# Context inverses: key products one group a step behind U, vector slack of two gaps, another filling of the head

## The chip, the cores and the metric

The kernel runs on one NeuronCore of a Trainium2 chip. The core has five engines that work side by side, each through its own queue of instructions: PE (TensorE, matrix products), DVE (VectorE), ACT (ScalarE), POOL (GpSimd) and SP (SyncE, which here only issues DMAs). The metric is the device time of one execution in microseconds (us).

## The reference

One layer of a hybrid backbone: 1024 latent tokens with a prefix of 256 context tokens, model width 1024. A modulated RMSNorm feeds one wide input projection, whose columns go to two branches: bidirectional RWKV-7 time mixing (16 heads of 64) and bidirectional retention. Both give gated outputs that are merged, projected and added to the input. The change concerns the RWKV-7 scan over the context. Per token the reference does

```python
sa = jnp.einsum('bhvk,bhk->bhv', S, kk_t)
S = (S * w_t[:, :, None, :] - sa[..., None] * b_t[:, :, None, :]
     + v_t[..., None] * k_t[:, :, None, :])
```

The latent scan starts from the final state S of the context scan of the same direction.

## The kernel before

**Chunks.** The scan is done in chunks of 64 tokens: 4 for the context, 16 for the latent tokens. Within a chunk the recurrence becomes a triangular system, and each chunk, head and direction needs the inverse T2 of a 64 x 64 triangular matrix. The states then pass from chunk to chunk by a few small products. There are 8 pairs of heads and 2 directions.

**Inverses.** One inverse job (`inverse(n)`, line 806) handles 64 such matrices in three stages, and is a Python generator. Each `yield` is a place at which the caller puts other work.
- `inv_keys` (line 847): loads keys from DRAM and makes four groups of key products (tile B on PE, 32 matmuls in the trace's records for each group). ACT evicts each group, in twelve copies, to the tiles D (line 883) and T (line 885). The loads of a group are two of tile kt and four of tile bi, on the SP queue. The tiles kt and bi have two buffers each, and a group uses both, so the next group's loads wait until the products of the group before are done. It yields once after the first loads and once after each group.
- `inv_vec` (line 888): inverts the 32 x 32 diagonal blocks on DVE: transposes of D to E (line 896), 31 rounds of two operations on tmp and TL (lines 902 and 904), transposes to TD and TN (lines 908 and 912). E needs the whole of D, all four groups. The generator hands out estimated durations, 32.1 us in all, and `inverse` yields each time 4.2 us (`VEC`) have been handed out: seven times.
- `inv_join` (line 925): two rounds of small products (tile I on PE, 128 matmul records a round) with TN and T, with four evictions by ACT after each round (lines 944 and 946). All of TN is needed for the first. It yields after each round.

**Chain.** The context scan runs in two groups of 4 head pairs, and each in two halves: four calls of `chain_ctx` (line 1094). I call them runs 1 to 4. A run loads its operands and makes chunk products (A, bt), with projection work put between by `fill(2.0)`, and then takes 4 steps (`chain_step`, line 1042). A step is X on PE, copied by ACT to xs; U on PE, copied by ACT to uv; S on PE, added on DVE to the state sv (line 1083; send at the last step). Each waits for the one before. After each of the three products the step calls `step_inv`, which advances the current inverse to its next yield, and then `gap`, which fills the gap with projection work. Two runs have 24 such calls; what is left of the inverse then is done at once (`drain`).

**Which inverse runs where.** Inverse 0 is for the first group of the context; it runs ahead of run 1 with nothing but projection work beside it. I call this stretch the head. Inverse 1, for the second group, is advanced in runs 1 and 2. Inverse 2, for the first latent chunks, is advanced in runs 3 and 4. After run 4 the rest of the projection is done, and the latent part begins.

**Filling.** The projection work of this phase is 8 jobs of 240 matmuls (tile gv, 128 x 256) with the split of their weights into a high part (whi, ACT, line 659) and a low part (wlo, DVE, line 660). `fill(us)` emits matmuls by an estimate of 0.107 us each. In the head each yield gets 2.8 us (`HEAD`), the first 7.0 us. A `gap` gets an equal share of what is left, less 8 us (`HOLD`) kept for the end: `share = max(self.left - self.hold, 0.0) / max(self.gaps, 1)`, with 48 gaps in all. So what the head emits is taken from the gaps.

**Order.** PE executes in the order of the program: `mm` and `pin` chain each product to the one before. Vector work and evictions of the inverse are kept behind the last chain operation of their engine (`late`), and the chain's own operations have a higher priority for the scheduler (`URGENT`), so that they stand ahead of waiting vector work. SP, DVE and ACT keep the order that the scheduler gave them.

Of the kernel before, what the change touches and what calls it, by code (L numbers as in the profile page):

```python
# [50 lines left out]
HEAD = 2.8  # L51
# [77 lines left out]
class Kern:  # L129
# [676 lines left out]
    def inverse(self, n):  # L806

        job = {}
        for _ in self.inv_keys(n, job):
            yield  # L810
            yield
        us = 0.0
        for t in self.inv_vec(job):
            us += t
            if us > VEC:
                us = 0.0
                yield
        for _ in range(5):
            yield
        yield from self.inv_join(job)  # L820

    def rwkv_ctx(self):
        pds = [[(p, d) for p in range(4 * g, 4 * g + 4) for d in range(2)] for g in range(2)]
        for i, _ in enumerate(self.inverse(0)):
            self.fill(HEAD if i else 2.5 * HEAD)
        for g in range(2):
            self.inv = self.inverse(g + 1)
            for q in range(2):
                self.chain_ctx(pds[g][4 * q:4 * q + 4], self.t2[g][q])
            self.drain()  # L830
# [769 lines left out]
```

## Time and profile before

| what | value |
|---|---|
| runs shown | 2459.37 us median of 3 (2459.12 to 2461.17) |
| the profiled execution | 2467.66 us |
| its span, first to last instruction | 2465.6 us |
| mean granted clock of PE | 0.986 |
| the phase of the change, in the trace | 815.5 to 1154.9 us |
| head; run 1 (loading and steps); run 2; run 3; run 4 and rest | from 815.5; 917.1; 974.3; 1034.9; 1097.3 us |

A page of the profile gives the busy time of each engine and the chain of work that ended last. The trace behind it answers closer questions: sums over stretches of time, groups of instructions by line and tile, and the instructions of an engine in order of time, each with the idle time of the engine before it and what released it. Lines such as L902 are lines of the kernel. In names such as B<-kt,bi the tile that is written stands ahead of the arrow. The steps of run 4 begin at 1116.3 us, and its last U, at 1133.3 us, is followed by the first join of inverse 2.

### The profile page before, as it was taken

How to read it: one execution, taken by the hardware profiler on the slowest of the kernel's cores; microseconds unless marked ns; L12 is line 12 of the kernel's file. 1: busy time of each engine (PE TensorE's matmuls, PEld its weight loads, DVE VectorE, ACT ScalarE, POOL GpSimd, SP SyncE). 2: the span in 40 equal slices, each digit the busy share in tenths (PEclk: the TensorE clock that was granted, in tenths of full speed). 3: DMA queues.
4: the chain of work that ended last, by engine and by line, in shares of the span. 5: the costliest groups of instructions: out<-in, count | busy, mean ns of one | idle time of the engine just before them, and what ended most of it. 6: DMA issues, size and time to landing. Idle time of an engine off the chain costs nothing.

```text
span 2465.6 us, 55584 instructions
## 1 busy us (share of the span) xinstructions
PE 2356.7 (96%) x22224; PEld 1927.3 (78%) x22224; DVE 1570.7 (64%) x2774; ACT 1120.5 (45%) x2411; POOL 682.8 (28%) x852
## 2 busy tenths in 40 slices
PE   7999999999999999999999999999898998999998
PEld 4888888888888899988877787777666765688786
DVE  5486787786776153434777788776378557754644
ACT  6434344434444424344555555644366335533422
POOL 2221021112122122323234433434376345400000
PEclk9999999999999899989999999999999999999999
DMA  6154454454446525344667777766565655585542
GB/s 253 50 152 116 142 154 138 127 171 124 139 140 175 183 80 141 105 132 132 164 173 195 190 192 180 189 175 163 148 201 158 202 169 159 175 294 163 186 169 86
DMA packets 417908, 393.60 MB, mean 160 GB/s; under 512 B 217578, under 2 KB 320754, under 8 KB 414578
## 3 DMA queue, kind: packets, MB, share of 16 engines
q1 hardware_dynamic: 392818, 299.85, 41.5%
q0 software_dynamic: 23104, 87.05, 12.4%
q8 instruction: 175, 2.87, 0.5%
q10 hardware_dynamic: 1728, 3.15, 0.3%
q14 instruction: 83, 0.68, 0.1%
HBM read 268.82 MB, written 121.11 MB: 158 GB/s over the span
## 4 chain that ended last, share of the span: by engine, by line
PE 82%; DVE 5%; DMA 5%; issue 3%; ACT 2%; POOL 1%; SPq 1%; DVEq 0%; ACTq 0%; POOLq 0%
PE gm L557 10%; PE gm L330 9%; PE gm L331 9%; PE gm L332 9%; PE gv L557 9%; PE ro L1479 4%; PE A L557 3%; PE yr L1279 2%; PE yr L1280 2%; PE yr L1278 2%; PE X L557 2%; PE bt L1038 2%; PE S L557 1%; PE O L557 1%; PE I L557 1%
## 5 line engine op out<-in xcount | busy, mean ns | idle before, releaser
L330 PE MATMUL gm<-uh,wh 128*128 128x512 f32 x896 | 351.2, 393 | 6.2 <-ACT xp L402 4.2
L331 PE MATMUL gm<-ul,wh 128*128 128x512 f32 x896 | 351.6, 392 | 0.8 <-DVE ul L299 0.8
L332 PE MATMUL gm<-uh,wl 128*128 128x512 f32 x896 | 351.2, 392 | 0.0
L330 PEld LDWEIGHTS gm<-uh,wh 128*128 128x128 f32 x896 | 168.1, 188 | 40.7 <-ACT xp L402 4.6
L331 PEld LDWEIGHTS gm<-ul,wh 128*128 128x128 f32 x896 | 168.4, 188 | 37.9 <-issue 1.7
L332 PEld LDWEIGHTS gm<-uh,wl 128*128 128x128 f32 x896 | 168.3, 188 | 34.3
L557 PE MATMUL gm<-ul,whi 128*128 128x512 f32 x416 | 168.5, 405 | 1.6 <-issue 1.6
L557 PE MATMUL gm<-uh,wlo 128*128 128x512 f32 x416 | 166.8, 401 | 1.0 <-DVE wlo L660 1.0
L557 PE MATMUL gm<-uh,whi 128*128 128x512 f32 x416 | 166.7, 401 | 0.0
L660 DVE TENSOR_TENSOR wlo<-wraw,whi 128x256 fp32r<-128x256 f32 x168 | 82.4, 508 | 129.1 <-ACT whi L659 128.4
L557 PE MATMUL gv<-whi,uh 128*128 128x256 f32 x512 | 151.5, 296 | 0.0
L557 PE MATMUL gv<-whi,ul 128*128 128x256 f32 x512 | 149.7, 292 | 0.0
L557 PE MATMUL gv<-wlo,uh 128*128 128x256 f32 x512 | 149.1, 291 | 0.0
L211 DVE TENSOR_TENSOR lo<-raw,hi 128x512 fp32r<-128x512 f32 x128 | 92.9, 730 | 88.2 <-ACT hi L210 87.7
L210 ACT CAST hi<-raw 128x512 fp32r<-128x512 f32 x128 | 78.6, 620 | 142.7 <-PE yr L1279 78.1
L1060 POOL TENSOR_TENSOR sp<-sv,pc 64x512 f32<-64x512 f32 (+1 forms) x92 | 89.5, 973 | 175.4 <-DVE sv L1083 153.9
L904 DVE TENSOR_TENSOR TL<-TL,tmp 128x31 f32<-128x31 f32 (+15 forms) x310 | 125.9, 406 | 8.2
L1479 PE MATMUL ro<-s,rs 128*128 128x512 f32 x256 | 124.5, 599 | 5.1 <-DVE s L1433 4.6
L902 DVE TENSOR_TENSOR tmp<-E,TL 128x31 f32<-128x31 f32 (+15 forms) x310 | 117.0, 377 | 8.4
L210 ACT CAST wh<-wr 128x1024 fp32r<-128x1024 f32 x56 | 58.8, 1050 | 130.6 <-PE gm L331 103.0
L456 POOL DMA_DIRECT2D vtD<-vt x64 | 46.1, 767 | 240.5 <-ACT vt L452 240.5
L1433 DVE SCALAR_TENSOR_TENSOR s<-s,ph,st 128x512 f32<-128x512 f32 x128 | 91.1, 739 | 33.8 <-PE st L1420 29.0
(300 smaller groups left out, 6217.5 us busy)
## 6 DMA issues: line engine op xcount, KB each, us to landing
wr<-in_w_in SPq DMA_DIRECT2D x56, 512.0 KB, 3.7
wraw<-in_w_in SPq DMA_DIRECT2D x84, 256.0 KB, 4.0
bk<-bkD SPq DMA_DIRECT2D x80, 256.0 KB, 4.3
krD<-kr POOLq DMA_DIRECT2D x16, 1024.0 KB, 4.6
raw<-in_wr SPq DMA_DIRECT2D x64, 256.0 KB, 3.3
vtD<-vt POOLq DMA_DIRECT2D x64, 160.0 KB, 4.2
bkD<-bk POOLq DMA_DIRECT2D x32, 320.0 KB, 6.6
bkD<-bk POOLq DMA_DIRECT2D x16, 640.0 KB, 6.5
```

What stands on the lines that cost most here:

```text
L210: nc.scalar.copy(hi, src)
L211: (eng or nc.vector).tensor_tensor(lo, src, hi.bitcast(F32), op=ALU.subtract)
L330: nc.tensor.matmul(acc[:, :n], hi[:, k, :], self.hi(k, t0, n), start=(k == 0), stop=False)
L331: nc.tensor.matmul(acc[:, :n], hi[:, k, :], self.lo(k, t0, n), start=False, stop=False)
L332: nc.tensor.matmul(acc[:, :n], lo[:, k, :], self.hi(k, t0, n), start=False, stop=(k == KT - 1))
L557: return self.pin(self.nc.tensor.matmul(*a, **k))
L660: self.late(nc.vector.tensor_tensor(lo[:, j % size, k:k + 2], r, h.bitcast(F32), op=ALU.subtract), "v")
L902: self.late(nc.vector.tensor_tensor(t3, et[:, j + 1:, j:j + 1].broadcast_to([P, n, m]), tl[:, j:j + 1, 0:m].broadcast_to([P, n, m]), op=AL ...
L904: self.late(nc.vector.tensor_tensor(tl[:, j + 1:, 0:m], tl[:, j + 1:, 0:m], t3, op=ALU.subtract), "v")
L1060: nc.gpsimd.tensor_tensor(sp[ch], sv[ch, h], pcs[ch].broadcast_to([64, m, C]), op=ALU.mult)
L1433: nc.vector.scalar_tensor_tensor(new[:, k], old[:, k], self.cd[:, d, h:h + 1], a, op0=ALU.mult, op1=ALU.add)
L1479: nc.tensor.matmul(po, qx[d][:, k, cols], st[:, k, :], start=(d == 1 and k == 0), stop=False)
```

## The change

Three numbers change. In `inverse`, the yields after the stages of `inv_keys` become 4, 3, 3, 3 and 1 in place of 2 each; the pause between vector work and join becomes 2 yields in place of 5. In `rwkv_ctx`, the filling of the head becomes 2.8 us for each of its first 14 pieces and 1.7 times as much, 4.76 us, for those after them, in place of 7.0 us for the first and 2.8 for the rest.

```diff
-        for _ in self.inv_keys(n, job):
-            yield
-            yield
+        for i, _ in enumerate(self.inv_keys(n, job)):
+            for _ in range((4, 3, 3, 3, 1)[i]):
+                yield
...
-        for _ in range(5):
-            yield
+        yield
+        yield
         yield from self.inv_join(job)
...
-            self.fill(HEAD if i else 2.5 * HEAD)
+            self.fill(HEAD if i < 14 else 1.7 * HEAD)
```

Counted in calls of `step_inv`: before, the groups of key products came at calls 3, 5, 7 and 9 (all in the first of the two runs, behind S, U, X and S), the vector work from call 11 to 18, and the join at call 23 and 24. Now the groups come at calls 5, 8, 11 and 14 (behind U of steps 2, 3 and 4 of the first run and of step 1 of the second), the vector work from call 15 to 22, the first round of the join at call 24, behind the last S, and the second in the drain.

In numbers of projection products on PE: the four groups of the head are 52 or 53 products apart before and 78 or 79 now; between the last of them and the first join there were 366 and are 426; a gap of runs 1, 2, 3 and 4 held about 22, 19, 15 and 6 and now holds 18 or 19, 15 or 16, 10 or 11, and 2. After the first round of inverse 2's join there were 6 + 3 + 6 + 72 products, and now there are 6 + 5 + 66.

PE at the last group of key products of inverse 2. Before, run 3, step 3 (S of that step, then the group; gv are projection products):

```order
L557 MATMUL gv_10255<-whi_9149,uh_98 128x256
L557 MATMUL S_10297<-uv_10060,bt_9738 64x64 x2
L557 MATMUL S_10297<-uv_10060,bt_9774 64x64 x2
L557 MATMUL S_10297<-uv_10060,bt_9830 64x64 x2
L557 MATMUL S_10297<-uv_10060,bt_9871 64x64 x2
L557 MATMUL B_10308<-kt_10229,bi_10230 64x64 x2
L557 MATMUL B_10309<-kt_10234,bi_10235 64x64 x2
```

The same group now, in step 1 of run 4:

```order
L557 MATMUL X_10687<-sv_10467,ka_10567 64x64 x2
L557 MATMUL gv_10586<-whi_9567,uh_104 128x256
L557 MATMUL gv_10586<-wlo_9568,uh_104 128x256
L557 MATMUL U_10703<-xs_10696,T_883_8350 64x64 x8
L557 MATMUL B_10714<-kt_10406,bi_10407 64x64 x2
L557 MATMUL B_10715<-kt_10411,bi_10412 64x64 x2
```

The group moved from behind S in run 3, ahead of the chunk loading of run 4, to behind U in run 4.

PE at the first round of the join of inverse 2. Before, in the last step of run 4, where a gap holds six products:

```order
L557 MATMUL gv_10961<-whi_9793,uh_98 128x256
L557 MATMUL gv_10961<-wlo_9794,uh_98 128x256
L557 MATMUL gv_10961<-whi_9793,ul_106 128x256
L557 MATMUL gv_10961<-whi_9793,uh_99 128x256
L557 MATMUL gv_10961<-wlo_9794,uh_99 128x256
L557 MATMUL gv_10961<-whi_9793,ul_107 128x256
L557 MATMUL U_10986<-xs_10975,T_870_8126 64x64 x8
L557 MATMUL I_10997<-TN_10865,T_1081_9945 32x32 x2
L557 MATMUL I_10998<-TN_10865,T_1082_9946 32x32 x2
```

Now, at the same place of the program:

```order
L557 MATMUL gv_10748<-whi_9567,uh_102 128x256
L557 MATMUL gv_10748<-wlo_9568,uh_102 128x256
L557 MATMUL U_10994<-xs_10984,T_883_8350 64x64 x8
L557 MATMUL gv_10748<-whi_9567,ul_110 128x256
L557 MATMUL gv_10748<-whi_9567,uh_103 128x256
L557 MATMUL S_11007<-uv_10879,bt_10522 64x64 x2
L557 MATMUL S_11007<-uv_10879,bt_10558 64x64 x2
L557 MATMUL S_11007<-uv_10879,bt_10606 64x64 x2
L557 MATMUL S_11007<-uv_10879,bt_10645 64x64 x2
L557 MATMUL I_11018<-TN_10962,T_1086_10056 32x32 x2
L557 MATMUL I_11019<-TN_10962,T_1087_10057 32x32 x2
```

The join moved from behind the last U to behind the last S, and the gaps ahead of it shrank from six products to two.

DVE at the start of the vector work of inverse 2. Before, in run 3 (sv are the state adds of its second and third step, wlo a split of projection weights):

```order
L1083 TENSOR_TENSOR sv_10059<-S_10163,sp_10076 64x256 x2
L660 TENSOR_TENSOR wlo_9794<-wraw_9901,whi_9793 128x256
L660 TENSOR_TENSOR wlo_9794<-wraw_10089,whi_9793 128x256
L1083 TENSOR_TENSOR sv_10191<-S_10297,sp_10208 64x256 x2
L896 STREAM_TRANSPOSE E_10399<-D_9944 128x256 x4
L660 TENSOR_TENSOR wlo_9794<-wraw_10089,whi_9793 128x256
L902 TENSOR_TENSOR tmp_10406<-E_10399,TL_10400 128x31
```

Now, in run 4 (ka are masked chunk products of its loading, sv the state add of its first step):

```order
L1014 TENSOR_TENSOR ka_10524<-A_10594,mask 64x256 x2
L1014 TENSOR_TENSOR ka_10567<-A_10633,mask 64x256 x2
L1083 TENSOR_TENSOR sv_10681<-S_10750,sp_10698 64x256 x2
L896 STREAM_TRANSPOSE E_10761<-D_10055 128x256 x4
L902 TENSOR_TENSOR tmp_10768<-E_10761,TL_10762 128x31
L904 TENSOR_TENSOR TL_10762<-TL_10762,tmp_10768 128x31
```

The start of the vector work moved from behind the third step of run 3 to behind the first step of run 4, past the loading of run 4.

## The prediction

> **What bounds the kernel now.** The page comes first: how busy each engine is, and who holds the chain of work that ended last.
>
> ```profile
> PE 2356.7 (96%) x22224; PEld 1927.3 (78%) x22224; DVE 1570.7 (64%) x2774; ACT 1120.5 (45%) x2411; POOL 682.8 (28%) x852
> PE 82%; DVE 5%; DMA 5%; issue 3%; ACT 2%; POOL 1%; SPq 1%; DVEq 0%; ACTq 0%; POOLq 0%
> ```
>
> TensorE is the bound, and it runs its instructions in the order written. The change adds and removes no product; it only moves products between places. So the question is how much TensorE time the context phase loses, before and after. The second view gives sums over stretches of time (length, busy time and instructions of PE, PEld, DVE, ACT and POOL, granted clock, DMA share, GB/s). Its last row is the whole phase, from the first projection product to the first product of the latent part; the others are the stretches at half clock inside it that a stall began.
>
> ```profile
> 839.60:846.43 6.83, 5.26 (x46) 5.09 (x47) 0.00 (x0) 3.22 (x12) 0.00 (x0) 0.50 0.66 196
> 1068.30:1075.12 6.82, 6.41 (x61) 5.96 (x62) 0.83 (x2) 3.22 (x12) 0.00 (x0) 0.50 0.58 165
> 1085.36:1092.19 6.83, 5.58 (x57) 5.13 (x57) 1.51 (x3) 3.22 (x12) 0.30 (x1) 0.50 0.48 120
> 1136.56:1146.80 10.24, 9.97 (x233) 8.79 (x232) 0.84 (x2) 4.06 (x9) 3.15 (x4) 0.50 0.51 117
> 815.50:1154.86 339.36, 324.53 (x4160) 305.35 (x4160) 135.65 (x349) 133.15 (x360) 83.74 (x117) 0.94 0.44 123
> ```
>
> PE idles 339.36 - 324.53 = 14.8 us of the phase. Half of the busy time at half clock is lost as well: (5.26 + 6.41 + 5.58 + 9.97) / 2 = 13.6. Together **28.4 us** is lost now, and that is all the change could win here. The third view, PE's rows in order of time, says who is waited for (idle time and releaser in brackets). I call the four calls of chain_ctx runs 1 to 4, and the inverses 0 (head), 1 (beside runs 1 and 2) and 2 (beside 3 and 4).
>
> ```profile
> 830.42 0.69 PE L557 MATMUL B<-kt,bi 64*64 64x64 f32 x32
> ...
> 841.17 1.45 PE L557 MATMUL B<-kt,bi 64*64 64x64 f32 x28 [3.36 <-DMA bi<-bkD]
> 850.80 0.69 PE L557 MATMUL B<-kt,bi 64*64 64x64 f32 x32
> 857.85 0.69 PE L557 MATMUL B<-kt,bi 64*64 64x64 f32 x32
> 902.58 0.75 PE L557 MATMUL I<-TN,T 32*32 32x32 f32 x64
> ...
> 955.43 1.00 PE L557 MATMUL B<-kt,bi 64*64 64x64 f32 x28 [1.23 <-DMA bi<-bkD]
> ...
> 1066.42 0.32 PE L557 MATMUL B<-kt,bi 64*64 64x64 f32 x2 [0.33 <-DMA bi<-bkD]
> 1067.33 0.33 PE L557 MATMUL B<-kt,bi 64*64 64x64 f32 x2 [0.58 <-DMA bi<-bkD]
> 1068.71 1.11 PE L557 MATMUL B<-kt,bi 64*64 64x64 f32 x26 [1.06 <-DMA bi<-bkD]
> 1086.61 1.11 PE L557 MATMUL B<-kt,bi 64*64 64x64 f32 x26 [1.82 <-DMA bi<-bkD]
> 1135.85 0.94 PE L557 MATMUL I<-TN,T 32*32 32x32 f32 x64 [1.86 <-DVE TN L912]
> ```
>
> Two kinds of wait: key products (B) for their operands from DRAM, and once a join (I) for the vector work that ends in TN. At 1135.85 PE stood still although 6 and then 72 ready projection products were queued behind the join: what stands behind a blocked product waits too.
>
> **What the wider spacing is worth.** A group's loads start when the group before has freed the two buffers. From the end of one B (850.80 + 0.69) to the next at 857.85, 6.4 us was enough; the loads that ended the wait at 955.43 were begun after a B that ended some 8.5 us earlier.
>
> ```profile
> 947.14 0.40 SPq L839 DMA_DIRECT2D kt<-kcD  x1
> ```
>
> So a group needs 6.4 to 8.5 us. In the head the spacing goes from 52 products to 79. The 366 products from 858.54 to 902.58 took 0.120 us each, so this is 9.5 us, against the 10.1 us from the first B's end (831.11) to 841.17, where its SP queue still had run 1's loads to issue: I leave 0.5 us of the 3.36, and no half clock. In run 1 three gaps of 18 products give about 8.4 us: 0.5 us is left. In run 3 the gaps shrink, since the head has taken their filling. A gap with 15 products and one with 6:
>
> ```profile
> 1054.39 0.69 PE L557 MATMUL X<-sv,ka 128*64 128x64 f32 x16
> 1056.99 0.68 PE L557 MATMUL U<-xs,T 64*64 64x64 f32 x16
> ...
> 1121.12 0.69 PE L557 MATMUL X<-sv,ka 128*64 128x64 f32 x16 [0.17 <-issue]
> 1122.64 0.68 PE L557 MATMUL U<-xs,T 64*64 64x64 f32 x16
> ```
>
> These are 2.60 and 1.52 us. By the new order run 3 has 10 or 11 products a gap, 2.07 us; three gaps leave 6.2 us between groups, so two groups wait 0 to 2.3 us each. I take the middle, 1.2 each, **2.4 us**, and no half clock, as the single wait of 1.23 us brought none. Its other end, 7.5 us, is two full waits and one half-clock stretch (2.9).
>
> **What the later last group costs.** The vector work starts from D, which the last group fills. Before, inverse 2's last group stood behind S in run 3, and the chunk loading of run 4 lay within the vector work's time. A sum over its stretch (length, PE busy, clock, DMA):
>
> ```profile
> 1097.20:1116.20 19.00, 19.00 (x203) 1.00 0.41 116
> ```
>
> This is 19 us of PE work that no longer covers it. The last group now stands behind U of the first step of run 4; inverse 1's likewise in run 2. How long the vector work takes, from the groups of DVE in the stretch of inverse 2 (busy, mean ns, idle before), then of inverse 0:
>
> ```profile
> L904 DVE TENSOR_TENSOR TL<-TL,tmp 128x31 f32<-128x31 f32 (+15 forms) x31 | 12.0, 388 | 1.0
> L902 DVE TENSOR_TENSOR tmp<-E,TL 128x31 f32<-128x31 f32 (+15 forms) x31 | 11.8, 380 | 0.9
> L1083 DVE TENSOR_TENSOR sv<-S,sp 64x256 f32<-64x256 f32 x6 | 2.5, 422 | 4.0 <-PE S L557 3.9
> L908 DVE STREAM_TRANSPOSE TD<-TL 128x256 f32<-128x256 f32 x4 | 2.4, 626 | 0.0
> L896 DVE STREAM_TRANSPOSE E<-D 128x256 f32<-128x256 f32 x4 | 2.2, 597 | 6.4 <-ACT D L883 6.4
> L912 DVE STREAM_TRANSPOSE TN<-TL 128x256 f32<-128x256 f32 x4 | 2.1, 614 | 0.0
> ...
> L902 DVE TENSOR_TENSOR tmp<-E,TL 128x31 f32<-128x31 f32 (+15 forms) x31 | 10.6, 343 | 1.0
> L660 DVE TENSOR_TENSOR wlo<-wraw,whi 128x256 fp32r<-128x256 f32 x10 | 3.8, 418 | 2.4 <-ACT whi L659 2.4
> ...
> 1090.68 2.15 DVE L896 STREAM_TRANSPOSE E<-D 128x256 f32<-128x256 f32 x4 [6.41 <-ACT D L883]
> ```
>
> Inverse 2: 12.0 + 11.8 + 2.4 + 2.2 + 2.1 + 1.9 between them = 32.4 us; inverse 0, with 10.6 in place of each of the two long rows, 30.1. I take **31**, and both ends for the range. E began 3.0 us after its last B ended (1086.61 + 1.11 = 1087.72), when ACT had evicted D.
>
> Inverse 2, from the end of its last B: 3.0 + 31 + three pairs of state adds (sv, sv, send) at 0.85 = 36.6 us to TN. By the new order a gap of run 4 holds 2 products: 1.52 - 4 x 0.12 = 1.04 us of PE work. Ten gaps to the end of run 4 are 10.3 us, and then the join is next on PE. So PE loses **26.3 us**, some 9 in run 4 (where X waits for a state add behind vector work on DVE) and the rest at the join. The second join product now follows the first directly and waits for ACT's four evictions, which a row of ACT prices:
>
> ```profile
> 1139.41 2.43 ACT L944 ACTIVATE T<-I 32x512 f32<-32x512 f32 x4 [2.30 <-PE I L557]
> ```
>
> This adds **2.3 us**. The 66 projection products left at the end, and the latent part's first A, B and gate products, are queued behind.
>
> Inverse 1: run 2 has 15 or 16 products a gap, 2.65 us, and ten gaps from the end of B to the join, 26.5 us. DVE's order puts E behind the first step's state add: 2.65 + 1.0. Then 31, seven weight splits (wlo) at 0.42 = 2.9, three pairs of adds 2.6, and 1.5 for adds that wait for S (0 to 3): TN is there after 41.6 us. PE waits **15.1 us**, with run 3's weights, chunk products and the whole of run 3 behind it. Inverse 0 does not wait: 426 products (51 us) now stand between its last B and its join, where 366 sufficed.
>
> Such waits end at half clock: after the first 5.3 busy us as at 839.60, **2.7 us** lost; after inverse 2, with the stop between its joins, 10 us as at 1136.56, **5.0 us**. The Trainium skill, "TensorE: Matmul & The Clock Gate", section "What's actually happening", has an idle window of about 3.4 us lower the clock and one busy window restore it. The stretches here are indeed two and three times 3.41 us, but the wait of 1.86 us sufficed to begin one; by the page's single window the two waits would lose about 3.4 us in place of 7.7, and the sum would be 22.
>
> **The sum.** After: 0.5 + 0.5 + 2.4 + 15.1 + 2.7 + 26.3 + 2.3 + 5.0 = 54.8 us lost; before 28.4. That is **+26.4 us**. The profiled execution took 2467.66 us (span 2465.6); it becomes 2494. The runs shown have a median of 2459.37, 8.3 lower, so I forecast 2459.4 + 26.4 = **2486 us**. Head and run 1 alone win 6 to 7 us; the two joins lose five times that. Moved ACT and SP work (twelve evictions and six loads a group, the same number as before) goes with its group; the copy of U stands ahead of the evictions on ACT in the new order, so the chain isn't held by them.
>
> **The rivals.**
> - *Slack suffices (faster).* If PE's gaps were as long as the vector work needs, only the gains would count: 1.0 + 2.4 + what the end of run 4 loses today (1.86 + 9.97 / 2 = 6.8), 10.2 against 28.4, giving 2441. It decides at 4 us a gap (41.6 over ten); the rows have 2.65 and 1.04. Chance 0.03.
> - *The two errors meet (no change).* Gains as said, half clock as said (1.0 + 2.4 + 7.7 + 2.3 = 13.4), and at the joins 15 us of waiting, a third of what I say: 28.4 lost as before, 2459. Against it speaks the wait of 1.86 us that is there today, with 19 us more of cover. 0.04.
> - *One join is covered.* If run 2's real gaps were 1.5 us longer than by the rows (ACT late with U or X), inverse 1 would wait nothing: 2486 - 17.8 = 2468. 0.08.
> - *More half clock.* Run 4 idles half its time; if the clock falls there and in run 3 and stays low through both joins, with full B waits, 5 + 5 + 5 more: 2500. Rows for it: the clock fell after 0.33 + 0.58 + 1.06 us of idling in a few us. [...] 0.10.
> - *The forecast*, 2476 to 2497: 0.75.
>
> **How the numbers follow.** Ends of the unknowns: vector work -0.9 to +1.4 for each inverse, adds -1.5 to +1.5, B waits -2.4 to +5.1, half clock -4.3 to +5. The range 2467 to 2500 takes these in and the covered join. Faster by over 0.2% (below 2454.5, about what a measurement can tell): 0.03; within: 0.04; slower: 0.93.
>
> **What would show it.** Right: in the profile after, the join of inverse 2 has an idle time before it of 14 us or more, released by TN on DVE, and that of inverse 1 of 10 or more; the wait for bi at 841 is gone; the four stretches of half clock move to behind the joins. Wrong: joins with less than 5 us before them, or the phase from first projection to first latent product under 345 us.

## The result, and the profile after

The changed kernel takes **2485.01 us** (median of 4 runs, 2482.62 to 2488.47), the kernel before 2459.24 us on the same chip (4 runs, 2457.64 to 2461.17). The ratio is 1.0093, with a 95% interval of 1.0079 to 1.0108, so the change costs 19 to 27 us. The profiled execution after took 2488.47 us, its span is 2486.7 us, and the mean granted clock is 0.982.

First the page of the kernel after, the busy time of the engines and the chain of work that ended last:

```profile
PE 2350.8 (95%) x22224; PEld 1923.3 (77%) x22224; DVE 1571.3 (63%) x2774; ACT 1120.4 (45%) x2411; POOL 681.1 (27%) x852
PE 82%; DVE 7%; DMA 5%; ACT 3%; issue 2%; POOL 1%; SPq 1%; DVEq 0%; ACTq 0%; POOLq 0%
```

The products are the same 22224, and no engine got more work. What moved is the chain: DVE's share rises from 5 to 7% of the span and ACT's from 2 to 3%. Next the sums over stretches of the kernel after, with the columns of the prediction's second view. The first row is the whole phase, the next two are its stretches at half clock behind the opening.

```profile
816.33:1179.40 363.07, 322.13 (x4160) 303.09 (x4160) 136.34 (x349) 133.44 (x360) 82.77 (x117) 0.91 0.41 115
1036.42:1053.49 17.07, 6.53 (x147) 6.18 (x148) 9.77 (x29) 4.82 (x8) 2.42 (x4) 0.50 0.13 39
1128.58:1172.95 44.37, 22.68 (x404) 19.05 (x403) 29.73 (x73) 9.37 (x18) 9.72 (x14) 0.50 0.29 70
```

The phase is 363.07 - 339.36 = 23.7 us longer; everything outside it is 2.6 us shorter, 2123.6 in place of 2126.2 us. (That is the same part of the program in every kernel of this study, and took between 2120.9 and 2134.1 us in their profiles.) Within the phase PE idles 363.07 - 322.13 = 40.9 us (14.8 before), and half of the busy time at half clock is (6.53 + 22.68) / 2 = 14.6 us (13.6 before). Lost together: 55.5 us after, 28.4 before. The change added idle time to PE. (The profiled execution before, at 2467.66 us, was 8.4 us above its median, the one after, at 2488.47 us, 3.5 above; that is why the traces differ by less than the medians, which are 25.8 us apart.) The rows of PE in order of time say where (idle time and releaser in brackets):

```profile
833.43 0.69 PE L557 MATMUL B<-kt,bi 64*64 64x64 f32 x32
843.73 0.69 PE L557 MATMUL B<-kt,bi 64*64 64x64 f32 x32
...
916.12 0.75 PE L557 MATMUL I<-TN,T 32*32 32x32 f32 x64
...
1006.32 0.63 PE L557 MATMUL B<-kt,bi 64*64 64x64 f32 x30
...
1046.96 1.08 PE L557 MATMUL I<-TN,T 32*32 32x32 f32 x64 [13.52 <-DVE TN L912]
...
1089.33 0.78 PE L557 MATMUL B<-kt,bi 64*64 64x64 f32 x28 [0.25 <-DMA bi<-bkD]
...
1097.59 0.29 PE L557 MATMUL B<-kt,bi 64*64 64x64 f32 x2 [1.13 <-DMA bi<-bkD]
1098.42 0.68 PE L557 MATMUL B<-kt,bi 64*64 64x64 f32 x26 [0.54 <-DMA bi<-bkD]
...
1121.61 0.63 PE L557 MATMUL B<-kt,bi 64*64 64x64 f32 x30
...
1126.90 0.68 PE L557 MATMUL U<-xs,T 64*64 64x64 f32 x16 [1.40 <-ACT xs L1056]
...
1160.50 1.08 PE L557 MATMUL I<-TN,T 32*32 32x32 f32 x64 [18.59 <-DVE TN L912]
...
1164.84 0.31 PE L557 MATMUL I<-T 32*32 32x32 f32 x2 [0.67 <-ACT T L944]
1165.45 0.31 PE L557 MATMUL I<-T 32*32 32x32 f32 x2 [0.30 <-ACT T L944]
```

The head is clean: no key product waits for bi, and the first inverse's join doesn't wait for TN. Both other joins do, 13.5 and 18.6 us. The rows of DVE show that it isn't slow; it starts late and is full until TN is done:

```profile
1125.70 1.60 DVE L896 STREAM_TRANSPOSE E<-D 128x256 f32<-128x256 f32 x3 [1.41 <-ACT D L883]
...
1157.85 0.61 DVE L908 STREAM_TRANSPOSE TD<-TL 128x256 f32<-128x256 f32 x1
1158.32 2.13 DVE L912 STREAM_TRANSPOSE TN<-TL 128x256 f32<-128x256 f32 x4
```

The last key product of inverse 2 ends at 1121.61 + 0.63 = 1122.24, TN is done at 1160.45: 38.2 us, of which 34.75 are DVE's, from E's start.

### The profile page after: what moved, and what is told of

Same layout as the page of the kernel before. It is cut to its first block, busy times and chain, and to the rows that moved or that the text cites. A ratio compares the mean times of both kernels' runs of the same rounds, so it can differ in the third digit from the quotient of the medians.

```text
span 2486.7 us, 55586 instructions
## 1 busy us (share of the span) xinstructions
PE 2350.8 (95%) x22224; PEld 1923.3 (77%) x22224; DVE 1571.3 (63%) x2774; ACT 1120.4 (45%) x2411; POOL 681.1 (27%) x852
## 4 chain that ended last, share of the span: by engine, by line
PE 82%; DVE 7%; DMA 5%; ACT 3%; issue 2%; POOL 1%; SPq 1%; DVEq 0%; ACTq 0%; POOLq 0%
PE gm L557 10%; PE gv L557 10%; PE gm L330 9%; PE gm L331 9%; PE gm L332 9%; PE ro L1479 3%; PE A L557 2%; PE yr L1279 2%; PE yr L1280 2%; PE yr L1278 2%; PE X L557 2%; PE S L557 1%; PE bt L1038 1%; PE O L557 1%; PE U L557 1%
## 5 line engine op out<-in xcount | busy, mean ns | idle before, releaser
L1026 DVE TENSOR_TENSOR ka<-A,mask 64x256 f32<-64x256 f32 x128 | 53.3, 416 | 96.4 <-PE A L557 95.3
```

Of the source, the lines that this page charges most:

```text
L1026: nc.vector.tensor_tensor(ka[va, 2 * h], pa[va, :, h], strict(va), op=ALU.mult)
```

## The experiments

My theory was that the last key group, now behind the second run's loading, starts the vector work too late, and PE stands at the join for what it can't cover. The first rival was that the filling is the cause: the head takes more projection work and run 4's gaps become thin. Two more were that the waits at the two joins are one delay which moves along, and that the time is lost in run 4's chain and only shows at the join. All ratios are to the kernel before on the same chip. Its median there was 2463.84 us for the first four, 2465.27 for the next three and 2461.70 for the last, so ratios are to be compared and not times. Each kernel's trace is of one execution, so a difference of a few us between two traces can be that of the executions; single executions of the kernel before went from 2454.8 to 2477.1 us in the second of these.

**The filling alone.** The kernel before, with the new filling of the head only:

```diff
-            self.fill(HEAD if i else 2.5 * HEAD)
+            self.fill(HEAD if i < 14 else 1.7 * HEAD)
```

> The kernel before with the new filling of the head alone; the groups of key products stay at calls 3, 5, 7 and 9. Theory P (position: the last group behind the loading of the second run leaves the vector work uncovered) expects no wait at inverse 1's join; the first B of the head 39 products (4.7 us) earlier but its second group's loads no sooner, so 4.7 us more idle there; the B groups of run 3 at 2.2 us gaps wait some 2.5 us more; run 4 at 1.16 us a gap makes inverse 2's join wait 3 to 4 us more: 2470 us. Rival F (filling: the gaps thinned by the head are what costs) expects nearly all of the loss: 2485 us.

Measured: 1.0002 (0.9985 to 1.0020). The new filling costs nothing that can be measured, so the rival falls, and so do the 2470 us that my own theory had for it. (By PE's rows a gap of run 4 holds three products here, where it holds two in the change.) Two views of this kernel tell why: PE's rows in the head and at inverse 2's join, then the sums over the last stretch at half clock.

```profile
834.11 0.43 PE L557 MATMUL B<-kt,bi 64*64 64x64 f32 x4 [0.46 <-DMA bi<-bkD]
834.92 0.29 PE L557 MATMUL B<-kt,bi 64*64 64x64 f32 x2 [0.38 <-DMA bi<-bkD]
835.82 0.67 PE L557 MATMUL B<-kt,bi 64*64 64x64 f32 x26 [0.60 <-DMA bi<-bkD]
...
1135.56 1.08 PE L557 MATMUL I<-TN,T 32*32 32x32 f32 x64 [0.96 <-DVE TN L912]
```

```profile
1127.10:1147.60 20.50, 18.80 (x369) 16.14 (x369) 8.46 (x21) 8.92 (x18) 8.13 (x13) 0.50 0.55 126
```

With the groups early, the join waits 0.96 us although the gaps ahead of it hold three products. The stretch at half clock doubled (20.5 us in place of 10.2), which costs 18.80 / 2 - 9.97 / 2 = 4.4 us, so thin gaps aren't free. The filling pays for it ahead of that: in the head the wait of 3.36 us for bi falls to 0.46 + 0.38 + 0.60 = 1.4, and the three earlier stretches at half clock, one in the head and two in run 3, last 3.41 us each in place of 6.83.

**The yields alone.** The change, with the head's filling of before:

```diff
-            self.fill(HEAD if i < 14 else 1.7 * HEAD)
+            self.fill(HEAD if i else 2.5 * HEAD)
```

> The changed kernel with the head's filling of before. Theory P expects the joins to wait still, less by what the thicker gaps cover: inverse 1 9.6 us for 13.5, inverse 2 some 4 us less, and a new wait of about 7 us with half clock at inverse 0's join, whose last group is now only 262 products (31.6 us) ahead of it: 2484 us. Rival F expects the loss to be gone: 2459 us.

Measured: 1.0105 (1.0080 to 1.0130), the whole loss. PE's rows of this kernel:

```profile
904.72 0.75 PE L557 MATMUL I<-TN,T 32*32 32x32 f32 x64 [3.82 <-DVE TN L912]
...
1039.72 1.08 PE L557 MATMUL I<-TN,T 32*32 32x32 f32 x64 [10.94 <-DVE TN L912]
...
1116.88 0.63 PE L557 MATMUL B<-kt,bi 64*64 64x64 f32 x30
...
1156.39 1.08 PE L557 MATMUL I<-TN,T 32*32 32x32 f32 x64 [20.46 <-DVE TN L912]
```

All three joins wait for TN. The first row is what the change's new filling is good for: without it the head's inverse waits too, 3.8 us where some 7 were expected. Inverse 2's join missed the expectation: it was to wait some 4 us less than in the change, for run 4's gaps are thicker here (five or six products), and it waits longer, 20.5 us for 18.6. From the last key product (1116.88 + 0.63) PE came to it after 18.4 us, in the change after 19.7: run 4 ran mostly at full clock here, and that took away at least the cover that the thicker gaps gave.

**The groups early again.** The change, but inverses 1 and 2 get their groups three calls earlier (2, 5, 8 and 11 in place of 5, 8, 11 and 14). The later spacing is kept, the last group stands in the first run again, and the join keeps its place by a longer pause:

```diff
-            for _ in range((4, 3, 3, 3, 1)[i]):
+            for _ in range((1 if n else 4, 3, 3, 3, 1)[i]):
...
-        yield
-        yield
+        for _ in range(5 if n else 2):
+            yield
```

> The changed kernel with the first group of inverses 1 and 2 three calls earlier (calls 2, 5, 8, 11: all behind U in the first of the two runs, ahead of the second run's loading) and the pause lengthened to 5 so that the join stays at call 24; inverse 0 and the whole filling as in the change. Theory P expects inverse 1's join not to wait, inverse 2's to cost about 7 us of idling in run 4 and at the join in place of 26, three B waits of 1.2 us in run 3: 2451 us, below the kernel before. Rival F (same thin gaps) expects 2485 us.

Measured: 1.0004 (0.9990 to 1.0019). The loss is gone, so it is the place of the groups, of which the last starts the vector work; but 2451 us were expected, and a gain over before is not there. PE's rows of this kernel at the end of run 4, ACT's at the same place, and the sum over the stretch at half clock there:

```profile
1118.65 1.12 PE L557 MATMUL X<-sv,ka 128*64 128x64 f32 x16 [2.58 <-issue]
...
1125.61 1.12 PE L557 MATMUL X<-sv,ka 128*64 128x64 f32 x16 [2.10 <-issue]
...
1132.67 1.12 PE L557 MATMUL S<-uv,bt 128*64 128x64 f32 x16 [3.43 <-ACT uv L1073]
1133.72 1.08 PE L557 MATMUL I<-TN,T 32*32 32x32 f32 x64
```

```profile
1126.83 0.38 ACT L1056 ACTIVATE xs<-X 128x256 f32<-128x256 f32 x1 [4.49 <-PE X L557]
1129.36 2.50 ACT L917 COPY T<-TD 32x512 f32<-32x512 f32 x4 [2.14 <-DVE TD L908]
1131.87 0.74 ACT L1073 COPY uv<-U 64x256 f32<-64x256 f32 x2
```

```profile
1125.50:1146.00 20.50, 15.38 (x332) 13.36 (x333) 6.31 (x17) 8.23 (x15) 7.94 (x12) 0.50 0.40 91
```

The join no longer waits, but the chain does: the last S stands 3.43 us for uv, whose copy ACT holds behind four copies of T that waited for DVE. The three waits are 8.1 us, and the clock then is at half for 20.50 us, with 15.38 / 2 = 7.7 us lost; before, the end of run 4 lost 1.9 us of waiting and 5.0 by half clock. So what the wider spacing and the covered join win goes there.

**Half of the vector work.** The change without 15 of the 31 rounds of vector work in inverses 1 and 2; every second round is kept, so the kernel leaves out part of these inverses:

```diff
+            if j % 2 == 0 or not job.get("half"):
```

> The changed kernel without 15 of the 31 rounds of vector work in inverses 1 and 2 (their inverses are then not computed); all places of products and gaps are unchanged. Theory P expects about 12 us less vector work each: inverse 1's join waits 1 us with no half clock, inverse 2's chain and join lose 14 us in place of 26: 2458 us. Rival F, in which the gaps and not the vector work set the time, expects 2485 us.

Measured: 1.0000 (0.9982 to 1.0018). The groups stand as late as in the change, and with less vector work the loss is gone, as expected: inverse 1's join doesn't wait for TN, and that of inverse 2 only

```profile
1137.95 1.07 PE L557 MATMUL I<-TN,T 32*32 32x32 f32 x64 [7.09 <-DVE TN L913]
```

by PE's rows of this kernel. So a late start and the vector work's length make the loss together.

**The left products ahead of the join.** The change, but inverse 2's join comes whole after run 4, behind all projection products that were left. By PE's rows these are 77: the 66 of the expectation, and the 11 that stood between the join's products.

```diff
-        yield
-        yield
+        for _ in range(2 + n // 2):
+            yield
...
+            if g:
+                self.fill(self.left)
             self.drain()
```

> The change, except that inverse 2's join comes whole after run 4's last step, and the projection products that are left (66, some 8 us at full clock) are put ahead of it in place of behind it; nothing is left out. Theory (PE waits for the vector work, and ready products queued behind the join could have run meanwhile): the 18.6 us wait at inverse 2's join falls to about 8 to 10, since the 66 products run inside it; the end of the vector work stays where it is, some 37 us after the last key group of inverse 2. About 9 us less than the change: 2476 where the change takes 2485 (1.2% becomes 0.5 to 0.7% over before). Inverse 1's wait stays at 13 to 14 us. Rival (the time is lost in run 4's chain, and the join's wait only shows where it ends): no gain, 2485, with the wait at the join still over 15 us or moved to the latent part's first products.

Measured: 1.0074 (1.0046 to 1.0102), a little above the 0.5 to 0.7% expected, which lie within the interval. The two waits in PE's rows:

```profile
1048.83 1.08 PE L557 MATMUL I<-TN,T 32*32 32x32 f32 x64 [13.51 <-DVE TN L914]
...
1162.66 1.93 PE L557 MATMUL I<-TN,T 32*32 32x32 f32 x128 [8.20 <-DVE TN L914]
```

Inverse 2's wait fell from 18.6 to 8.2 us, and inverse 1's is unchanged. The wait is idle time that ready products could fill, and they only stood behind the join. (The intervals of this run and of the change overlap; the rows carry the reading.)

**Only inverse 1 early.** The change, with the early groups for inverse 1 alone:

```diff
-            for _ in range((4, 3, 3, 3, 1)[i]):
+            for _ in range((1 if n == 1 else 4, 3, 3, 3, 1)[i]):
...
-        yield
-        yield
+        for _ in range(5 if n == 1 else 2):
+            yield
```

> The change, except that inverse 1 alone has its key groups three calls earlier (calls 2, 5, 8, 11, so the last of them stands in run 1) and a pause of 5 calls ahead of its join; inverse 0, inverse 2 and the filling are the change's. Nothing is left out. Theory (each inverse loses by its own late last group): inverse 1's wait of 13.5 us and the half clock behind it (6.5 / 2 = 3.3) go, inverse 2's 18.6 us and the long half-clock stretch behind it stay: 16.8 less than the change, 2468 where the change takes 2485 and before 2459; the price that the prediction gave the case of one covered join. Rival (the two waits are one delay that moves along, so that what inverse 1 doesn't wait inverse 2 does): 2480 to 2485, with more than 25 us before inverse 2's join.

Measured: 1.0041 (1.0021 to 1.0061), where 1.0037 was expected. In PE's rows of this kernel inverse 1's first join products stand without a wait, and inverse 2's as late as in the change:

```profile
1035.93 0.75 PE L557 MATMUL I<-TN,T 32*32 32x32 f32 x64
...
1148.78 1.08 PE L557 MATMUL I<-TN,T 32*32 32x32 f32 x64 [17.08 <-DVE TN L912]
```

So the two waits are separate, each with its own price, and the delay does not move along.

**Early groups, and less filling in the head.** The kernel with the early groups, with 1.3 in place of 1.7, which leaves run 4 four or five products a gap:

```diff
-            self.fill(HEAD if i < 14 else 1.7 * HEAD)
+            self.fill(HEAD if i < 14 else 1.3 * HEAD)
```

> Inverses 1 and 2 with key groups at calls 2, 5, 8 and 11 and a pause of 5 calls, as in the run of that name, and the later pieces of the head at 1.3 in place of 1.7 times the projection, so that run 4 has 4 or 5 products a gap in place of 2. Nothing is left out. Theory (the run with early groups lost 8 us in run 4, where gaps of 2 products don't cover ACT's copies, and 10 us by half clock behind that): run 4's waits fall to 3 us or less, the half-clock stretch behind them to 10 us or less, and the head's inverse still has enough products before its join (332 against the 30 us of vector work); phase 332 to 336 us, 3 to 6 us faster than before, ratio 0.9975 to 0.9988. Rival (the loss at the end of run 4 comes from ACT's evictions beside the chain whatever the gaps hold, or inverse 0 now waits): within 2 us of before.

Measured: 0.9979 (0.9962 to 0.9997). PE's rows, and the sums over the stretch at half clock at the join and over the phase:

```profile
1111.26 0.69 PE L557 MATMUL X<-sv,ka 128*64 128x64 f32 x16 [0.93 <-issue]
1116.63 0.69 PE L557 MATMUL X<-sv,ka 128*64 128x64 f32 x16 [0.97 <-PE gv L557]
1127.40 1.08 PE L557 MATMUL I<-TN,T 32*32 32x32 f32 x64 [7.27 <-DVE TN L912]
```

```profile
1121.90:1139.00 17.10, 10.02 (x276) 8.84 (x277) 5.25 (x10) 6.70 (x12) 6.07 (x10) 0.50 0.34 78
816.73:1146.19 329.46, 315.04 (x4160) 296.80 (x4160) 142.19 (x349) 133.90 (x360) 83.63 (x117) 0.96 0.46 127
```

Run 4's waits fell under 1 us each, as expected, and the phase is shorter than the 332 to 336 us that I had. Of the 9.3 us against the run with early groups, 322.41 - 315.04 = 7.4 are PE's busy time, that is clock:

```profile
813.81:1152.57 338.76, 322.41 (x4161) 303.03 (x4161) 139.21 (x349) 133.48 (x360) 82.89 (x117) 0.94 0.44 123
```

This row is the phase of the run with early groups. What I hadn't expected is the join: PE now reaches it sooner than DVE, and waits 7.3 us. The half clock that begins in this wait lasts 17.1 us, where 10 or less were expected.

**Both together.** That kernel, and in it inverse 2's join behind the products that are left:

```diff
-        for _ in range(5 if n else 2):
+        for _ in range(5 + n // 2 if n else 2):
...
+            if g:
+                self.fill(self.left)
             self.drain()
```

> The run with early groups and 1.3 times the projection in the head's later pieces, and in it inverse 2's join comes whole after the projection products that are left, as in the run that put these products first. Nothing is left out. Theory (in the run it starts from, PE still stood 7.3 us ahead of inverse 2's join with the left products ready behind it, and 2.3 us between its rounds): the 7.3 us fall under 1, and the half-clock stretch of 17 us behind run 4 shortens or goes: 6 to 10 us less than that run, ratio to before 0.9940 to 0.9960. Rival (the left products were the cover of the join's evictions and of the latent part's first products, so the wait moves behind the join): no gain, ratio 0.997 to 0.999.

Measured: 2450.57 us (8 runs) against 2461.70 us before, **0.9959** (0.9943 to 0.9975), as expected: 0.4% faster than the kernel before, and faster than the change. PE's rows at the join and at the latent part's start, and the sums over the phase and over a stretch at half clock behind it:

```profile
1128.09 1.29 PE L557 MATMUL I<-TN,T 32*32 32x32 f32 x128
1130.03 0.24 PE L557 MATMUL I<-T 32*32 32x32 f32 x2 [0.65 <-ACT T L946]
...
1135.48 1.12 PE L557 MATMUL A<-ka,bk 64*64 64x128 f32 x12 [1.50 <-issue]
1138.08 0.48 PE L557 MATMUL B<-kt,bi 64*64 64x64 f32 x4 [1.49 <-ACT T L948]
```

```profile
815.84:1133.04 317.20, 309.81 (x4161) 292.13 (x4161) 143.33 (x352) 133.51 (x361) 82.48 (x114) 0.99 0.48 133
1133.70:1143.90 10.20, 6.50 (x60) 4.74 (x52) 2.52 (x8) 6.32 (x19) 2.64 (x5) 0.50 0.41 114
```

The wait for TN is gone, and with it the long stretch at half clock: 309.81 us busy, a mean clock of 0.99, 7.4 us idle. A part comes back behind the phase, as the rival said: two waits of 1.5 us, and 6.50 / 2 = 3.3 us by half clock. The phase is 22.2 us shorter than before, where the medians differ by 11.1. Most of the rest lies in the two executions that were profiled: that of before, 2467.66 us, was 6.0 us above the median of before given here, and that of this kernel, 2446.93 us, was its shortest and 3.6 us below its median. Outside the phase, with these two waits and the half clock in it, this kernel is 1.7 us longer by the two traces.

The phase in all of them, from the row of the whole phase (idle is length less PE's busy time):

| kernel (one execution each) | phase, us | PE idle, us | wait at inverse 1's, 2's join | ratio to before |
|---|---|---|---|---|
| before | 339.4 | 14.8 | none, 1.9 | 1 |
| the change | 363.1 | 40.9 | 13.5, 18.6 | 1.0093 |
| filling alone | 338.6 | 12.4 | none, 1.0 | 1.0002 |
| yields alone | 359.3 | 40.0 | 10.9, 20.5 | 1.0105 |
| groups early | 338.8 | 16.4 | none, none | 1.0004 |
| half the vector work | 339.2 | 17.4 | none, 7.1 | 1.0000 |
| left products first | 350.9 | 31.9 | 13.5, 8.2 | 1.0074 |
| only inverse 1 early | 349.8 | 28.7 | none, 17.1 | 1.0041 |
| early, less head | 329.5 | 14.4 | none, 7.3 | 0.9979 |
| both together | 317.2 | 7.4 | none, none | 0.9959 |

## Why the prediction was right

The forecast was 2486 us, and 2485.01 us came. That the two are 1 us apart is luck in part: the interval of the loss runs from 19 to 27 us, and terms that were too high made up for others that were too low, as the list shows. The mechanism is the one that it named, and the runs show it from three sides: earlier groups take the loss away, so does a shorter vector work, and products that are put ahead of the join fill the wait. Term by term:

- **Head and run 1, 0.5 us each.** No wait for bi in either. Right. For run 1 the forecast's own row would have given no wait: three gaps of 18 products are 3 x (2.60 + 3 x 0.12) = 8.9 us, not 8.4, and 8.5 were enough.
- **Key products of run 3, 2.4 us.** 0.25 + 1.13 + 0.54 = 1.9. Right, and without half clock.
- **Inverse 1, 15.1 us of waiting.** 13.5. From its last key product (1006.32 + 0.63) to the end of TN it took 40 us, where I had 41.6; the 26.5 us for PE's ten gaps came out as predicted. Right.
- **Inverse 2, 26.3 us, 9 of them in run 4.** At the join 18.6, in run 4 about 3.7, together 22.3: the wait at the join was about right (17 said), that in run 4 was too high. Sums over the time from the last key product to the join, and over what follows it at half clock, for the kernel after:

```profile
1122.24:1160.50 38.26, 15.70 (x182) 12.29 (x181) 33.32 (x82) 9.37 (x27) 9.07 (x13) 0.58 0.42 101
1160.50:1172.95 12.45, 10.87 (x280) 9.69 (x281) 0.00 (x0) 5.15 (x9) 2.63 (x5) 0.50 0.01 3
```

  I had 36.6 us to TN with 10.3 us of PE work in it. It was 38.3 with 15.7, since the clock fell early in run 4 and PE's products took longer (1.12 in place of 0.69 us for the 16 of an X). But DVE sets the end of this stretch, so by this reading those longer products cost nothing; they only turned idle time into busy time.
- **Half clock, 2.7 + 5.0 us.** By the sum over stretches it is 14.6. Counted where PE sets the pace, behind the joins, it is 6.53 / 2 + 10.87 / 2 = 8.7, close to the 7.7 of the text. The remaining 11.82 / 2 = 5.9 us lie in DVE's shadow, by the sum from where the clock fell to the join:

```profile
1128.58:1160.50 31.92, 11.82 (x125) 9.36 (x123) 29.73 (x73) 4.21 (x10) 7.09 (x10) 0.50 0.40 96
```

  Counted as waiting, they make 40.9 + 5.9 = 46.8 us of it against my 47.1, and 8.7 of half clock against 7.7.
- **Second round of the join, 2.3 us.** 0.67 + 3 x 0.30 = 1.6. (ACT's row gave 2.43 us for the four copies; its 2.30 is ACT's idle time.)
- **The sum, 54.8 us.** 55.5 by the same count. Taken like this, every term is within 2 us. The head, runs 1 and 3, inverse 1 and the second round were too high by 3.8 us together; inverse 2, with those 5.9 us, and half clock were too low by 2.9, and 1.6 us of small idle times were left out. So the sum's closeness is luck, the size of its two main terms is not.
- **The way of counting.** Half of the busy time at half clock is too much: the 64 products at a join take 0.75 us at full clock and 1.08 at half, those of an X 0.69 and 1.12, so 31 and 38% are lost. As the busy time at half clock is nearly the same before and after (27.2 and 29.2 us), the difference hardly suffers. But the counts differ by 55.5 - 28.4 = 27.1 us where the phase grew by 23.7, and the 3.4 us between them stay open.
- **Vector work of inverse 0, 30.1 us.** With 10.6 in place of both long rows it is 29.8; the forecast doesn't hang on it.
- **One join covered, 2468 us.** It didn't happen here; the kernel with inverse 1 early is that case, and 1.0041 times 2459.24 is 2469. The rival's price was right.
- **More half clock, 2500 us.** Its premise came true in part: the clock fell in run 4 and stayed low through inverse 2's join, 44.4 us; in run 3 it didn't fall, and the B waits weren't full. Its price for run 4 didn't come, for the reason above. The forecast's own sign, that half clock moves to behind the joins, failed there as well: this stretch began 32 us ahead of its join.

Why the clock stays low is not settled by these runs. In the kernel with the filling alone it stayed at half for 20.50 us, in which PE was busy for 18.80 us, and from 1137.34 to 1140.75 us without a break. The Trainium skill, "TensorE: Matmul & The Clock Gate", section "What's actually happening", has one busy window of about 3.4 us restore it. The stretch is six such windows long, so here the measurement differs from the page.

Two expectations missed the time, both on what the filling's thin gaps do. The filling alone was priced at 2470 us and cost nothing that can be measured: inverse 2's join waited 0.96 us, not the 5 to 6 expected, and the longer half clock was paid for earlier. The early groups were to come to 2451 us and won nothing: the chain's copy on ACT queued behind the inverse's, and the thin gaps of run 4 were no cover for it. The kernel with 1.3 in the head, where these waits are gone, fits the second part.

## What to carry to other kernels

When a piece of work on another engine must be done by a fixed point of TensorE's order, count the TensorE time between the product that starts it and the product that needs it; moving the start past a block of loading takes that block's whole time out of the cover, here 19 us, and a join behind it then holds up every ready product. If the cover can't be had, put the ready products ahead of the join. And count lost clock only where TensorE sets the pace; here that is a reading of the sums, which no run tried by itself.

## What the runs showed of the hardware

- The granted clock stayed at half for 44.37 us, with PE busy for 22.68 us of it in short groups, and for 44.40 us again where inverse 1 was early, busy 22.71 us, by the sums over the same kind of stretch in that kernel:

```profile
1116.60:1161.00 44.40, 22.71 (x403) 19.08 (x404) 29.96 (x75) 9.61 (x19) 9.74 (x14) 0.50 0.31 73
```

- PE needn't idle much for that: the stretch of 20.50 us in the kernel with the filling alone has 18.80 us of busy time. What it was busy with were mostly short products in small groups; that this is the reason was not tried by itself.
- The long stretch began within run 4 in all six kernels with two or three projection products a gap there (at 1128.58 us in the change). In the four kernels with four to six a gap, none longer than 3.41 us began within run 4. The number of products in the gaps was never changed alone, so this is no proof.
